# Position-weight sums by VectorE through DRAM, norm rows loaded inside the loop, high parts first: one change to a two-layer gMLP and mLSTM trunk

## The chip, the cores and the metric

The kernel runs on one core of a Trainium2 chip, in one launch. The metric is the device time of that launch in microseconds (us). A core has five engines with their own instruction streams: TensorE (PE in the profile; its weight loads are listed apart as PEld), VectorE (DVE), ScalarE (ACT), GpSimd (POOL) and SyncE (SP). SP does no arithmetic here; it issues nearly all DMA transfers, in order, and an instruction that waits holds up what stands behind it on its engine. On-chip memory has 128 partitions: tiles live in SBUF, and matmuls write to PSUM, which has eight banks.

## The reference

The input is 256 tokens of 1024 features in float32. Two layers follow one another. Layer 0 mixes tokens with a chunked causal gMLP, layer 1 with an mLSTM of 4 heads; after each come a SwiGLU block of width 2816 and a gated embedding. Every sub-block ends in a layer norm over alpha * x + y. The part that the change speaks of first is the gMLP:

```python
z = jax.nn.gelu(x @ w_in)
u, v = jnp.split(z, 2, axis=-1)
v = layer_norm(v, ln_g, ln_b)
ws = jnp.where(causal, w_s, jnp.zeros_like(w_s))
sv = jnp.einsum('gts,bcsgd->bctgd', ws, v) + b_s.T[:, :, None]
return (u * sv.reshape(B, S, GM_HALF)) @ w_out
```

There are 8 groups of 384 features, and chunks of 128 positions. Since v is normalised with gain and bias per feature, the kernel applies the position weights to the plain normalised v, scales by the gain, and adds bias times R plus b_s. R[g, t] is the sum of the masked position weights ws[g, t, s] over s.

## The kernel before

**Precision.** All products are made in float32 by pairs: a value is split into a high part (a cast to TensorE's float32r format) and a low part (what the cast leaves over). A product is then three matmuls: high by high, low by high, high by low. The helper `split` (L151) makes both parts, the cast on ScalarE (or on VectorE with `fast`) and the subtraction on VectorE. So each weight goes through four steps: a DMA into a tile `raw` (4 buffers), the cast and the subtraction into a tile `w` (6 buffers, or 8 wider ones), and the matmuls.

**The stream of weights.** `weight_plan` (L75) lists all weight tiles of 512 KB (a few are smaller) in the order of use. `ahead` (L170) issues loads up to 8 tiles ahead of use and splits up to 4 ahead; `weight` (L208) hands out the next tile. The loads are all issued by SP, L176. The first three weights are loaded and split by halves.

**The order of instructions.** The text gives each engine a program order, but a planner places the instructions: with its own estimate of times it lets a later instruction that could start go ahead of an earlier one that could not, and assigns buffers. `issue_after` holds a block's instructions behind a given one on the same engine, and `manual_schedule` keeps the text's order on the engines named.

**The start (L353 to L376).** Eight dummy matmuls warm TensorE up. x arrives transposed, in four tiles of two feature blocks (`xr`), and is split into `xh` and `xl`. The very first halves of x and of the first weight are cast by VectorE, the rest by ScalarE.

**The v phase (L379 to L412).** For six column groups c, the product x by the v half of w_in is accumulated over eight feature blocks k, for two token tiles t; then GELU and the statistics of the norm. At c = 4 the position weights arrive, transposed (`wsr`, s on the partitions, with t along the row); GpSimd zeroes the part over the diagonal, and they are split into `ws`. TensorE then multiplies a matrix of ones by them: each result has R for all t in every partition. ScalarE copies that into `R` (L393 to L398). `bs` is a row of 1024 values, spread over the partitions by its load. wsr, bs and R share three buffers with the tag "row", as the norm rows do.

**The u, gating and output loop (L482).** In step s, `u_block` makes 128 features of u, `sv_block` (L442) mixes positions for 128 features of v, and `acc.add` multiplies a finished block by w_out. In `sv_block` the moving operand has 256 columns, the high and the low part of `ws` side by side; there are two matmuls per token tile, one for the high part of v and one for its low part (L448). GpSimd makes `cf`, R times the bias plus b_s (L451, L452), and adds it.

**The channel mixer (L497), once in each layer.** `boundary` ends an accumulation with a layer norm, whose gain and bias are rows of 1024 that `load_row` (L347) spreads over the partitions, 512 KB each. `first` makes the first 512 features of gate and up by token tiles; the loop over f makes the others by `gate_up`, with `acc.add` of the down product two blocks behind. The rows for the second norm and for the embedding gate (g2, b2, bg, L582) are loaded, by the text, after that loop; the planner can place them earlier.

**The mLSTM's gates (L843 to L881).** After the q, k and v products come the gates of all heads: a short chain on VectorE and ScalarE over 4 partitions. Its results have to get to TensorE twice: `transpose_cols` (L860) turns them into columns, and `broadcast_gates` (L867) spreads G over the partitions with a 4-row selection matrix, two heads for each call. Both are put between the products of z block 10 (`z_mm(10, ...)`, L875): the number in the dictionary is the k before which a piece stands.

**The mLSTM's down product (L968 to L984).** `Down` accumulates into four PSUM banks, two for each token tile. At the beginning the first two blocks are multiplied for token tile 0, then for token tile 1; from f = 2 on, each block is done for both at once.

Of the kernel before, what the change touches and what calls it, by code (L numbers as in the profile page):

```python
# [133 lines left out]
def trunk(ctx, tc, a, out):  # L134
# [35 lines left out]
    def ahead(loads, casts):  # L170
        while at["load"] < min(len(plan), at["use"] + loads):
            ap = plan[at["load"]][1]
            n = ap.shape[-1]
            t = tl("raw", [P, n], name="raw")
            for c in HALF if at["load"] < 3 else [slice(0, n)]:
                sp.dma_start(t[:, c], ap[:, c])  # L176
                if at["load"] == 0 and c.start == 0:
                    second_x()
            raws[at["load"]] = t
            at["load"] += 1  # L180
        while at["cast"] < min(len(plan), at["use"] + casts):
# [12 lines left out]
            with issue_after(behind["cast"]):  # L194
# [6 lines left out]
                for c in () if key[0] == "bdv" else HALF if i < 3 else [slice(0, n)]:  # L201
                    split(t[:, 0, c], t[:, 1, c], raw[:, c], fast=i == 0 and c.start == 0)
# [156 lines left out]
    for i in range(4):  # L359
        t = tl("m2", [P, 2, S], name="xr")  # L360
        if i == 0:

            act.dma_start(t[:, 0, :], a["xT"][i, :, 0, :])
            second_x = lambda: sp.dma_start(xr[0][:, 1, :], a["xT"][0, :, 1, :])
            xr.append(t)
        else:
            sp.dma_start(t, a["xT"][i])
            xr.append(t)
        ahead(1 + i, int(i == 0))
    make_identity(nc, ident)  # L370
    pool.memset(mhalf, -0.5)
    for i in range(4):
        for k in ((0,), (1,)) if i == 0 else ((0, 1),):
            c, cr = slice(2 * i + k[0], 2 * i + k[-1] + 1), slice(k[0], k[-1] + 1)
            split(xh[:, c, :], xl[:, c, :], xr[i][:, cr, :], fast=c.start == 0)
            ahead(LOAD_AHEAD, 1 + i)  # L376

    vs = []
    for c in range(6):  # L379
        if c == 4:  # L380
# [11 lines left out]

            R = tl("row", [P, NG, P], name="R")  # L393
            for j in range(2):
                ps = bank("A", [P, 4, P], "rps")
                for i in range(2):
                    pe.matmul(ps, ones_r, ws[:, 4 * j:4 * j + 4, i, :], start=i == 0, stop=i == 1)
# [44 lines left out]
    def sv_block(f):  # L442
# [3 lines left out]
        for t in range(2):  # L446
            for i in range(2):
                pe.matmul(ps[:, t], v[:, i, t, c], ws[:, g], start=i == 0, stop=i == 1)  # L448
# [48 lines left out]
    def channel_mixer(l, acc, last, hook=None):  # L497
# [70 lines left out]
        transpose_h(0)  # L568
        for f in range(4, NF + LAG):
# [12 lines left out]
        g2, b2, bg = load_row(a["ln2_g"][l]), load_row(a["ln2_b"][l]), load_row(a["ple_b"][l])  # L582
# [94 lines left out]
    def mlstm(embed1):  # L677
# [156 lines left out]
        with tc.manual_schedule(engines={mybir.EngineType.Activation}):  # L834
# [32 lines left out]
            def broadcast_gates():  # L867

                gb = bank("A", [P, 2, 2, P], "gb")
                for h in range(2):  # L870
                    for i in range(2):
                        pe.matmul(gb[:, h], selH[:, 2 * len(gbs) + h, :], Gs[i], start=i == 0, stop=i == 1)
# [95 lines left out]
        acc = Down(NI)  # L968
        for h in range(NH):
# [22 lines left out]
def lay_out(inputs):  # L992
# [26 lines left out]
    def part(w):  # L1019
# [11 lines left out]
        "gm_wsT": i["gm_w_s"][0].transpose(2, 0, 1).reshape(P, NG * P),  # L1031
        "gm_bs": i["gm_b_s"][0].reshape(-1),
# [47 lines left out]
```

## Time and profile before

| What | Value |
|---|---|
| time before, median of 3 runs (lowest to highest) | 827.05 us (826.75 to 827.43) |
| profiled execution: its time, its span | 827.14 us, 825.4 us |
| granted TensorE clock in it | 0.999 |
| TensorE matmuls | 817.7 us busy, 4520 instructions |
| TensorE weight loads | 708.6 us |
| VectorE, ScalarE, GpSimd | 615.5, 471.4, 152.3 us |
| DMA | 155.52 MB, 188 GB/s on average |

The profile is of one execution. Its time and its span differ because the span runs from the first to the last instruction of the program. In a timeline row the columns are: start in us from the span's start, length in us (for several merged instructions, from the first start to the last end), engine, line of the kernel, operation, the tile written and the tiles read, shapes, and the number of instructions; in brackets stands the idle time of the engine before it and what ended it. A row with "q" at the engine is the engine's sequencer, such as SP issuing a DMA. In a row of waits come who waited, for whom, the total in us, the number of times and the longest. Matmuls overlap: each has a latency of its own, and the distance between two starts tells what one costs in a stream.

### The profile page before, as it was taken

The numbers are of one execution on the slowest core, as the hardware profiler recorded it, in microseconds if no ns is written. First come the engines' busy times: TensorE is split into PE (matmuls) and PEld (weight loads), VectorE is DVE, ScalarE is ACT, GpSimd is POOL, SyncE is SP. The second block draws the span as 40 slices with busy tenths as digits, with TensorE's granted clock in tenths as the row PEclk, the third lists the DMA queues.
The fourth block names the chain that finished last, engine by engine and source line by source line (L and its number), as shares of the span: only waits on it lengthen the run. The fifth ranks groups of instructions, "written<-read, shape, count | busy, mean of one in ns | idle before, by whom it ended". The sixth has DMA issues, their size and how long they took to land.

```text
span 825.4 us, 12401 instructions
## 1 busy us (share of the span) xinstructions
PE 817.7 (99%) x4520; PEld 708.6 (86%) x4520; DVE 615.5 (75%) x981; ACT 471.4 (57%) x819; POOL 152.3 (18%) x209
## 2 busy tenths in 40 slices
PE   9999999999999999999999999999999999999997
PEld 6888888888888888888889999998887888888886
DVE  6757998678956567596877998889785656776674
ACT  6656766565435556475256788776434555655522
POOL 1020633343000000700001777420000000000000
PEclk9999999999999999999999999999999999999999
DMA  8885456558286567577144454454636656886501
GB/s 303 277 329 179 153 169 215 179 183 290 93 282 196 179 192 261 185 250 235 47 135 160 134 165 154 166 180 151 229 124 220 195 180 193 257 247 220 179 1 52
DMA packets 44997, 155.52 MB, mean 188 GB/s; under 512 B 5256, under 2 KB 6024, under 8 KB 44936
## 3 DMA queue, kind: packets, MB, share of 16 engines
q1 hardware_dynamic: 44792, 154.60, 56.9%
q8 instruction: 35, 0.57, 0.3%
q14 instruction: 26, 0.21, 0.1%
q10 hardware_dynamic: 144, 0.13, 0.0%
HBM read 153.67 MB, written 1.05 MB: 187 GB/s over the span
## 4 chain that ended last, share of the span: by engine, by line
PE 95%; DVE 2%; DMA 1%; ACT 1%; issue 0%; SPq 0%; POOL 0%; DVEq 0%; ACTq 0%
PE acc L240 9%; PE acc L241 9%; PE acc L242 9%; PE pu L260 8%; PE pg L260 8%; PE ups L260 5%; PE pg L264 4%; PE pu L264 4%; PE ups L264 3%; PE vps L242 3%; PE vps L240 3%; PE vps L241 3%; PE xmps L245 2%; PE xmps L247 2%; PE xmps L246 2%; PE gate L289 2%
## 5 line engine op out<-in xcount | busy, mean ns | idle before, releaser
L153 DVE TENSOR_TENSOR w<-raw,w 128x1024 fp32r<-128x1024 f32 (+1 forms) x279 | 336.1, 1212 | 74.2 <-ACT w L153 72.9
L153 ACT CAST w<-raw 128x1024 fp32r<-128x1024 f32 (+1 forms) x278 | 286.6, 1042 | 118.9 <-PE acc L242 23.5
L240 PE MATMUL acc<-w,h 128*128 128x512 f32 x336 | 131.8, 392 | 0.2 <-ACT hn L943 0.2
L241 PE MATMUL acc<-w,h 128*128 128x512 f32 x336 | 131.4, 391 | 0.0
L242 PE MATMUL acc<-w,h 128*128 128x512 f32 x336 | 130.8, 389 | 0.0
L242 PEld LDWEIGHTS acc<-w,h 128*128 128x128 f32 x336 | 63.1, 188 | 13.6
L240 PEld LDWEIGHTS acc<-w,h 128*128 128x128 f32 x336 | 63.2, 188 | 12.3 <-ACT hn L943 0.6
L241 PEld LDWEIGHTS acc<-w,h 128*128 128x128 f32 x336 | 63.2, 188 | 10.9
L260 PE MATMUL pg<-xs,w 128*128 128x512 f32 x288 | 71.6, 391 | 0.0
L260 PE MATMUL pu<-xs,w 128*128 128x512 f32 x288 | 71.5, 390 | 0.0
L260 PEld LDWEIGHTS pg<-xs,w 128*128 128x128 f32 x288 | 53.8, 188 | 11.0
L260 PEld LDWEIGHTS pu<-xs,w 128*128 128x128 f32 x288 | 53.8, 188 | 11.0
L319 POOL TENSOR_TENSOR rs<-ve,mhalf 128x1 f32<-128x1 f32 x8 | 7.6, 956 | 297.3 <-DVE ve L318 292.8
L271 ACT COPY s<-pg 128x256 f32<-128x256 f32 x36 | 13.4, 372 | 73.3 <-PE pg L264 73.3
L272 DVE TENSOR_TENSOR s<-s,pg 128x256 f32<-128x256 f32 x36 | 15.1, 421 | 45.5 <-ACT s L271 45.4
L260 PE MATMUL ups<-xs,w 128*128 128x512 f32 x192 | 47.7, 391 | 0.0
L260 PEld LDWEIGHTS ups<-xs,w 128*128 128x128 f32 x192 | 35.7, 188 | 7.2
L264 PEld LDWEIGHTS pg<-xs,w 128*128 128x128 f32 x288 | 38.9, 188 | 3.1
L264 PE MATMUL pg<-xs,w 128*128 128x256 f32 x288 | 39.5, 280 | 0.0
L264 PE MATMUL pu<-xs,w 128*128 128x256 f32 x288 | 39.4, 279 | 0.0
L240 PE MATMUL vps<-w,xs 128*128 128x512 f32 x96 | 37.6, 392 | 0.5 <-DVE w L153 0.5
L241 PE MATMUL vps<-w,xs 128*128 128x512 f32 x96 | 37.5, 390 | 0.0
(245 smaller groups left out, 1625.6 us busy)
## 6 DMA issues: line engine op xcount, KB each, us to landing
raw<-in_ffn_g SPq DMA_DIRECT2D x44, 512.0 KB, 4.3
raw<-in_ffn_u SPq DMA_DIRECT2D x44, 512.0 KB, 4.3
raw<-in_ffn_d SPq DMA_DIRECT2D x44, 512.0 KB, 4.4
raw<-in_gm_u SPq DMA_DIRECT2D x24, 512.0 KB, 3.4
raw<-in_gm_wo SPq DMA_DIRECT2D x24, 512.0 KB, 3.3
raw<-in_gm_v SPq DMA_DIRECT2D x21, 512.0 KB, 4.9
raw<-in_ple_gate SPq DMA_DIRECT2D x16, 512.0 KB, 4.5
raw<-in_ml_z SPq DMA_DIRECT2D x16, 512.0 KB, 3.6
```

What stands on the lines that cost most here:

```text
L153: return dve.tensor_copy(hi, src) if fast else act.copy(hi, src), sub.tensor_tensor(lo, src, hi.bitcast(F32), ALU.subtract)
L240: pe.matmul(ps, lh, w[:, 0, c], start=start, stop=False)
L241: pe.matmul(ps, ll, w[:, 0, c], start=False, stop=False)
L242: pe.matmul(ps, lh, w[:, 1, c], start=False, stop=stop)
L245: pe.matmul(ps, w[:, 0, c], h, start=start, stop=False)
L246: pe.matmul(ps, w[:, 0, c], l, start=False, stop=False)
L247: pe.matmul(ps, w[:, 1, c], h, start=False, stop=stop)
L260: pe.matmul(ps, w[:, 0, k * P:(k + 1) * P], xs[:, k], start=k == 0, stop=False)
L264: pe.matmul(ps[:, 0], w[:, 1, k * P:(k + 1) * P], xh[:, k, :], start=False, stop=k == KD - 1)
L271: act.copy(o, ps[:, 1])
L272: dve.tensor_tensor(o, o, ps[:, 0], ALU.add)
L289: pe.matmul(ps, xl[:, k, TOK[t]], w[:, 0, c], start=False, stop=k == KD - 1)
```

## The change

1. **R.** The position weights are also loaded untransposed at c = 3 (`wsn`, t on the partitions). GpSimd zeroes the part over the diagonal, VectorE sums over s into a tile `Rt` of 128 x 8, a DMA issued by GpSimd writes this to a DRAM scratch `Rd` (8 x 128), and a second one loads it back, spread over the partitions, into `R`. The four matmuls by ones and the two copies of ScalarE go.
2. **Gating.** The matmul of v's low part takes only the high part of `ws`: 128 columns instead of 256. The product of the two low parts is left out.
3. **Norm rows.** g2, b2 and bg are loaded at f = 8, 10 and 12 inside the loop, each held on SP behind the weight load issued last.
4. **Gates.** The transposes stand before k = 2 instead of 1; the broadcasts of all four heads stand before k = 4, in one piece, instead of two before k = 4 and k = 7.
5. **Start.** On ScalarE and VectorE the splits of the first four blocks of x and of the first two weights are in an order written out by hand, with the casts shared out differently; in the first four blocks of the first product, each block's high by high matmuls come first, for both token tiles, then low by high, then high by low.
6. **Down product of the mLSTM.** It begins with three blocks for token tile 0, then three for token tile 1.

The core of the diff:

```diff
@@ trunk
+    with tc.manual_schedule(engines={mybir.EngineType.Activation, mybir.EngineType.DVE}):
+        for i in range(2):
+            w, raw = tl("w", [P, 2 * D + P], F32R, "w")[:, :2 * D].rearrange("p (i n) -> p i n", i=2), raws.pop(i)
+            for k, h in enumerate(HALF):
+                c = 2 * i + k
+                act.copy(xh[:, c], xr[i][:, k])
+                if k == 0:
+                    dve.tensor_copy(w[:, 0, h], raw[:, h])
+                else:
+                    act.copy(w[:, 0, h], raw[:, h])
+                dve.tensor_tensor(xl[:, c], xr[i][:, k], xh[:, c].bitcast(F32), ALU.subtract)
+                dve.tensor_tensor(w[:, 1, h], raw[:, h], w[:, 0, h].bitcast(F32), ALU.subtract)
+            wt[i] = w
...
     for c in range(6):
+        if c == 3:
+            wsn = tl("row", [P, NG, P], name="wsn")
+            sp.dma_start(wsn, a["gm_ws"].rearrange("p (g s) -> p g s", g=NG))
+            pool.affine_select(
+                out=wsn, in_=wsn, compare_op=ALU.is_ge, fill=0.0, base=0, pattern=[[0, NG], [-1, P]], channel_multiplier=1
+            )
+            Rt = tl("c", [P, NG], name="Rt")
+            dve.tensor_reduce(Rt, wsn, mybir.AxisListType.X, ALU.add)
+            Rd = ctx.enter_context(tc.tile_pool(name="dr", bufs=1, space=bass.MemoryType.DRAM)).tile([NG, P], F32, name="Rd")
+            pool.dma_start(Rd.rearrange("g t -> t g"), Rt)
+            R = tl("row", [P, NG, P], name="R")
+            pool.dma_start(R, Rd.rearrange("g t -> (g t)").partition_broadcast(P).rearrange("p (g t) -> p g t", g=NG))
...
-            R = tl("row", [P, NG, P], name="R")
-            for j in range(2):
-                ps = bank("A", [P, 4, P], "rps")
-                for i in range(2):
-                    pe.matmul(ps, ones_r, ws[:, 4 * j:4 * j + 4, i, :], start=i == 0, stop=i == 1)
-                act.copy(R[:, 4 * j:4 * j + 4, :], ps)
...
+                if c == 0 and k < 4:
+                    for x, i in ((xh, 0), (xl, 0), (xh, 1)):
+                        for t in range(2):
+                            pe.matmul(ps[t], x[:, k, TOK[t]], w[:, i, HALF[kk]], start=k == 0 and x is xh and i == 0, stop=False)
+                    continue
@@ sv_block
-            for i in range(2):
-                pe.matmul(ps[:, t], v[:, i, t, c], ws[:, g], start=i == 0, stop=i == 1)
+            pe.matmul(ps[:, t], v[:, 0, t, c], ws[:, g], start=True, stop=False)
+            pe.matmul(ps[:, t, 0], v[:, 1, t, c], ws[:, g, 0], start=False, stop=True)
@@ channel_mixer
+            if f in (8, 10, 12):
+                with issue_after([at["dma"]]):
+                    rows.append(load_row(a[("ln2_g", "ln2_b", "ple_b")[f // 2 - 4]][l]))
...
-        g2, b2, bg = load_row(a["ln2_g"][l]), load_row(a["ln2_b"][l]), load_row(a["ple_b"][l])
+        g2, b2, bg = rows
@@ mlstm
-                gb = bank("A", [P, 2, 2, P], "gb")
-                for h in range(2):
+                gbs.extend(bank("A", [P, 2, 2, P], "gb") for _ in range(2))
+                for h in range(NH):
                     for i in range(2):
-                        pe.matmul(gb[:, h], selH[:, 2 * len(gbs) + h, :], Gs[i], start=i == 0, stop=i == 1)
-                gbs.append(gb)
-            z = z_mm(10, {1: transpose_cols, 4: broadcast_gates, 7: broadcast_gates})
+                        pe.matmul(gbs[h // 2][:, h % 2], selH[:, h, :], Gs[i], start=i == 0, stop=i == 1)
+            z = z_mm(10, {2: transpose_cols, 4: broadcast_gates})
...
-                if f == 0:
-                    first = block
-                elif f == 1:
-                    for t in range(2):
-                        for b, h2, w in (first, block):
+                if f < 3:
+                    begin.append(block)
+                    for t in range(2) if f == 2 else ():
+                        for b, h2, w in begin:
                             acc.mm(b, t, h2, w)
```

More of the change, by code (lines that the diff above doesn't have):

```diff
@@ L201, in ahead @@
                 for c in () if key[0] == "bdv" else HALF if i < 3 else [slice(0, n)]:
-                    split(t[:, 0, c], t[:, 1, c], raw[:, c], fast=i == 0 and c.start == 0)
+                    split(t[:, 0, c], t[:, 1, c], raw[:, c])
             wt[i] = t
@@ L368, in trunk @@
             xr.append(t)
-        ahead(1 + i, int(i == 0))
+        ahead(1 + i, 0)
     make_identity(nc, ident)
     pool.memset(mhalf, -0.5)
[L372 to L376, printed above, removed]
+    with tc.manual_schedule(engines={mybir.EngineType.Activation, mybir.EngineType.DVE}):
[11 more added lines that the diff above has]
+            wt[i] = w
+    at["cast"] = 2
+    for i in range(2, 4):
+        c = slice(2 * i, 2 * i + 2)
+        split(xh[:, c, :], xl[:, c, :], xr[i])
+        ahead(LOAD_AHEAD, 1 + i)
     vs = []
     for c in range(6):
+        if c == 3:
[10 more added lines that the diff above has]
+            pool.dma_start(R, Rd.rearrange("g t -> (g t)").partition_broadcast(P).rearrange("p (g t) -> p g t", g=NG))
         if c == 4:
@@ L568, in channel_mixer @@
         transpose_h(0)
+        rows = []
         for f in range(4, NF + LAG):
@@ L968, in mlstm @@
         acc = Down(NI)
+        begin = []
         for h in range(NH):
```

3 lines of the change are left out of this document (2 added, 1 removed).

## The prediction

> **What bounds the kernel now.** I read the page's totals first, then TensorE's waits, then the timeline around each place that the diff touches. Three lines of the page: the span, the engines' busy times, the DMA packets of the main queue.
>
> ```profile
> span 825.4 us, 12401 instructions
> PE 817.7 (99%) x4520; PEld 708.6 (86%) x4520; DVE 615.5 (75%) x981; ACT 471.4 (57%) x819; POOL 152.3 (18%) x209
> q1 hardware_dynamic: 44792, 154.60, 56.9%
> ```
>
> TensorE works through the whole span; beside its own weight loads (86%) no engine is above 75%. So an edit counts by what it takes from TensorE's stream, or from the few moments in which that stream stands. All such moments after the start, by TensorE's waits:
>
> ```profile
> PE first L286 <- ACT w L153: 1.1, 1, 1.1
> PE acc L240 <- ACT hn L943: 0.2, 1, 0.2
> PE cp L863 <- DVE gt L853: 0.2, 1, 0.2
> ```
>
> They are short, and the listed wait understates each, because matmuls overlap: a row of a matmul lasts 0.39 us, while the next one starts 0.23 us later. I therefore cost everything by the distance from start to start. The profiled execution took 827.14 us, that is 1.74 us around its span and 0.09 us above the median of 827.05; I sum against 827.14 and take 0.09 off.
>
> **Part 1, the sums R.** The ones-matmuls in TensorE's timeline, and the first matmul behind them:
>
> ```profile
> 49.59 1.07 PE L397 MATMUL rps<-ws,ones_r 128*128 128x512 f32 x4
> 50.50 0.39 PE L240 MATMUL vps<-w,xs 128*128 128x512 f32 x1
> ```
>
> Four matmuls go, 50.50 - 49.59 = **0.91 us** (0.228 for each of 512 columns). Nothing waited for them or made them wait, so this is plain. Two copies by ScalarE go too, which is worth nothing: ScalarE is 57% busy. In their place come: a 512 KB load on SP's queue, a select of 128x1024 by GpSimd, a sum of 128x1024 by VectorE, a write of 1024 single 4-byte elements to DRAM and a 512 KB spread load, both issued by GpSimd. Rows that bound them, in order: the select of the same size, VectorE's pass of that size, the first use of R's products, the landing times of the row loads, and the issue and first use of the first u weight.
>
> ```profile
> 41.83 1.11 POOL L383 TENSOR_SCALAR_AFFINE_SELECT wsr<-wsr 128x1024 f32<-128x1024 f32 x1 [38.61 <-DMA wsr<-in_gm_wsT]
> L153 DVE TENSOR_TENSOR w<-raw,w 128x1024 fp32r<-128x1024 f32 (+1 forms) x279 | 336.1, 1212 | 74.2 <-ACT w L153 72.9
> 83.05 1.29 POOL L457 TENSOR_TENSOR sv<-sv,cf 128x256 f32<-128x256 f32 x1 [7.00 <-ACT sv L456]
> DMA to landing us min/median/max: 3.6/5.9/8.0
> 49.41 0.33 SPq L176 DMA_DIRECT2D raw<-in_gm_u  x1
> 72.42 1.82 PE ups L260 x8
> ```
>
> I let the new load take the place of wsr, so that the data are there at 41.8; the select takes 1.1, the sum about 1.2 (VectorE's mean for a pass over 128x1024), so 44.2. The write has no row like it. Lower bound 3.6 us, the shortest row load. Upper: 56.9% of 16 engines' 825.4 us over 44792 packets is 0.168 us a packet; 1024 packets on 16 engines are then 10.7 us, and 8.0 for landing. The spread load is 3.6 to 8.0. R lands between 51 and 71, nearer 55, as the two are ordinary small and large transfers; it is needed at 83. Cost zero, covered by 12 us at worst. The new waits: GpSimd stands before the spread load until the write has landed; behind it are the select of wsr, the cf products and at 83.05 the first sum, nothing else. VectorE's sum waits for the select; behind it are weight splits, and SP's load of bs waits for that sum because there are only three row buffers, with weight loads behind it. TensorE uses the first u weight 23 us after its load was issued, so delays of some us there are absorbed.
>
> **Part 2, the narrower gating matmuls.** 48 matmuls (24 blocks, two token tiles) go from 256 columns to 128. TensorE's and the weight loads' timeline; the first two rows are today's svps block and its successor, the others a place where a 272-column and a 136-column matmul alternate already:
>
> ```profile
> 80.58 0.64 PE L448 MATMUL svps<-ws,vn 128*128 128x256 f32 x4
> 81.05 0.86 PE L260 MATMUL ups<-xs,w 128*128 128x512 f32 x3
> 457.68 0.23 PE L775 MATMUL vps<-w,xm 128*128 128x136 f32 x1
> 457.74 0.34 PE L774 MATMUL vps<-w,xm 128*128 128x272 f32 x1
> 457.91 0.23 PE L775 MATMUL vps<-w,xm 128*128 128x136 f32 x1
> 457.68 0.19 PEld L774 LDWEIGHTS vps<-w,xm 128*128 128x128 f32 x1
> 457.79 0.19 PEld L775 LDWEIGHTS vps<-w,xm 128*128 128x128 f32 x1
> ```
>
> Today a 256-column matmul takes (81.05 - 80.58)/4 = 0.118 us. By columns, 128 would take 0.06, and indeed 457.74 - 457.68 = 0.06 behind the short one. But the long one behind it then stands 0.17 instead of 0.12: the pair takes 457.91 - 457.68 = 0.23, since the next weights cannot follow sooner than 457.79 - 457.68 = 0.11. A short matmul thus costs what a weight load costs, 0.11, and saves about 0.01: **0.5 us** in 48. Bounds: 0.3 (the pair at 0.23 against 0.236) and 48 x 0.06 = 2.9. I stay near the row with the same pattern. By the Trainium skill, "TensorE: Matmul & The Clock Gate", section "Back-to-back issue gap", a stream of load and matmul pairs sustains about 81 ns per matmul at 128 columns; by that this part would be an estimated 1.8 us. The trace disagrees with its 0.11, and the measurement decides.
>
> **Part 3, the norm rows.** SP's queue, the chain that ended last, TensorE in the second channel mixer, and the usual landing of such a weight:
>
> ```profile
> 611.78 0.33 SPq L349 DMA_DIRECT2D row<-in_ln_b  x1
> 612.57 0.33 SPq L349 DMA_DIRECT2D row<-in_ple_b  x1
> 613.70 5.96 DMA raw<-in_ffn_u
> 619.75 1.05 ACT w L153
> 619.31 0.39 PE L286 MATMUL first<-w,xs 128*128 128x512 f32 x1
> 620.84 0.50 PE L286 MATMUL first<-w,xs 128*128 128x512 f32 x1 [1.14 <-ACT w L153]
> 621.18 0.40 PE L287 MATMUL first<-w,xs 128*128 128x512 f32 x1
> raw<-in_ffn_u SPq DMA_DIRECT2D x44, 512.0 KB, 4.3
> ```
>
> Two row loads of 512 KB go out just before a weight that is already late (it had to wait for a buffer), and it lands after 5.96 us where 4.3 is usual; ScalarE's split of 1.05 follows. TensorE loses 620.84 - 619.31 - 0.23 = 1.3 us, and 0.1 more at the restart (621.18 - 620.84 = 0.34 for 0.23). With the rows gone from there the weight lands after 3.6 (the quickest row load, of the same size) to 4.3, at 617.3 to 618.0; the split ends by 619.1, before the 619.54 at which TensorE would want it, and the weights behind it are for later tiles. Gain **1.4 us**; zero if the landing still takes 5.9. The three loads of each layer (0.33 of issue each) now stand in SP's queue behind a weight of f = 8, 10 and 12, with the next weights behind them. TensorE has no wait in that loop and the transfers fill 57% of the engines' time; cost zero, cover the weights' lead; without it 0.33 and about 1.5 of transfer each. In the first layer the same move finds no stall to remove.
>
> **Part 4, the gate transposes and broadcasts.** TensorE in the z product of block 10:
>
> ```profile
> 528.39 0.28 PE L863 MATMUL cp<-ident,gt 4*128 4x4 f32 x2
> 528.84 0.28 PE L863 MATMUL cp<-ident,gt 4*128 4x4 f32 x2 [0.17 <-DVE gt L853]
> 530.10 0.28 PE L247 MATMUL zps<-xs,w 128*128 128x256 f32 x1
> 530.31 0.73 PE L872 MATMUL gb<-G,sel 4*128 4x256 f32 x4
> 531.20 0.28 PE L246 MATMUL zps<-xs,w 128*128 128x256 f32 x1
> ```
>
> One position later means three matmuls of 0.118 later, 0.35 us. The second pair stood 0.45 behind the first, with 0.17 of listed idle time; 0.35 later it finds its operand. A wait costs more than is listed (part 3); I take 0.23, half of the 0.45. A change to the four-row broadcasts and back costs: from 530.10 to 531.20 are six matmuls, 0.71 by columns but 1.10 in fact, so 0.39 per visit, and one of two visits goes. Together **0.6 us**, between 0 and 0.7.
>
> **Part 5, the start.** VectorE, ScalarE and TensorE, the first weights:
>
> ```profile
> 4.48 0.29 DVE L153 CAST xs<-xr 128x256 fp32r<-128x256 f32 x1 [3.03 <-DMA xr<-in_xT]
> 4.69 0.42 DVE L153 CAST w<-raw 128x512 fp32r<-128x512 f32 x1
> 5.17 0.50 PE L240 MATMUL vps<-w,xs 128*128 128x512 f32 x1 [0.50 <-DVE w L153]
> 7.94 1.32 ACT L153 CAST w<-raw 128x512 fp32r<-128x512 f32 x2
> 8.61 0.50 PE L240 MATMUL vps<-w,xs 128*128 128x512 f32 x1
> 11.52 0.39 PE L240 MATMUL vps<-w,xs 128*128 128x512 f32 x1
> ```
>
> VectorE makes both first casts one after the other; now ScalarE makes that of x, so the first matmul can start 0.2 earlier, and with the high products first the low parts are wanted 0.45 later each. That alone is not kept: the second weight's cast starts at 7.94, and TensorE goes on only at 8.61. VectorE's cast of a half (0.42) in place of ScalarE's (1.32 for two, 0.66) brings this to 8.4. From 8.61 to the 25th matmul at 11.52 another 0.18 is lost against twelve of 0.228. I take **0.25 us**; bounds: the 0.9 by which 24 matmuls exceed 24 x 0.228, and a loss of 0.1, one more restart, should a low part now be late.
>
> **Part 6, three blocks ahead in the down product:** zero, at most 0.4 (the wait on hn above). TensorE's order here is the planner's, not the text's, and I expect it to fill this wait as before.
>
> Sum: 0.91 + 0.5 + 1.4 + 0.6 + 0.25 = 3.66 us; 827.14 - 3.66 - 0.09 = **823.4 us**.
>
> **Rivals.** *The late weight stays late* (other transfers fill the gap, or the planner moves something else there): 1.4 less, 824.8. For it: the load starts only when a buffer is freed. Against: 5.96 is the outlier beside 4.3.
>
> *Short matmuls cost by columns*: 2.4 more than taken, 821.0. The start 0.06 behind the short one speaks for it, the 0.17 behind the next against. The figure of the Trainium skill in part 2 points this way; by it the whole would be an estimated 822.1.
>
> *R comes late, the kernel gets slower.* Place: the cf products that GpSimd must finish before 83.05. If the two transfers issued by GpSimd need over 39 us together (44.2 to 83), every us more is a us of TensorE's; at 43 the gain is gone, and at 46 the time is 830.4. For it: the trace has no transfer issued by GpSimd. Against: 27 us is the most that I can derive. By the Trainium skill, "SBUF — State Buffer", section "SBUF: two separate sides", GpSimd writes such a transfer's descriptors and is locked out while VectorE runs a two-port operation, for which a copy of f32 qualifies; no run here shows it yet.
>
> *The planner's new order opens other waits*, of the size of the 1.3 us one, in two or three places: 826 to 828, no change that can be told.
>
> **How the numbers follow.** Forecast 0.52, weight still late 0.20, by columns 0.08, R late 0.08, new waits 0.12. About 0.2% (1.65 us) is what a measurement of this kernel can tell from no change. Forecast, late weight and columns are faster, 0.80; new waits 0.12 the same; R late 0.08 slower. The range goes from 820.7, 0.3 under the columns' case, to 825.9, the sum of the lower bounds (827.05 - 0.91 - 0.3 + 0.1): it holds 0.80.
>
> **What would show it.** Right: no rps matmuls; svps pairs at 0.23 and weight loads 0.11 apart; no wait of "first" on w; one visit of gb; cp without a wait; TensorE's 25th matmul near 11.3. Wrong: svps pairs at 0.18, a wait of GpSimd's cf on R past 83, a new line above 0.5 us in TensorE's waits.

## The result, and the profile after

The changed kernel takes 835.41 us (median of 4 runs, 834.44 to 835.84); the kernel before took 826.90 us beside it (4 runs, 826.73 to 827.43). The ratio is 1.0095, with a 95% interval from 1.0083 to 1.0108: **slower by about 8.5 us**, where 823.4 us had been forecast. The profiled execution took 835.21 us, its span is 833.5 us.

The page's totals, span and busy times of the engines, after:

```profile
span 833.5 us, 12406 instructions
PE 820.8 (98%) x4516; PEld 710.4 (85%) x4516; DVE 614.5 (74%) x983; ACT 469.5 (56%) x818; POOL 152.3 (18%) x212
```

Four matmuls are gone, and yet TensorE is listed as 3.1 us busier. Matmuls that only run longer at a lower clock count as busy, so this line alone does not say where the time went. TensorE's waits do, in part (who waited for whom, total, times, longest, in us):

```profile
PE vps L240 <- ACT w L153: 3.1, 1, 3.1
PE svps L475 <- DVE vn L153: 2.1, 1, 2.1
PE vps L242 <- DVE w L153: 0.7, 1, 0.7
PE num L946 <- POOL plo L153: 0.4, 1, 0.4
```

The wait of `first` on a weight (1.1 us before) and the one of `cp` (0.2 us) have gone, as the prediction said. Four new lines have come. To place the whole difference I compared the starts of the same matmuls in the two timelines of TensorE:

| Stretch | Change in this stretch, us |
|---|---|
| up to the 25th projection product (vps) | -0.06 |
| to the last projection product | +5.21 |
| to the first mixing product (svps) | +0.05 |
| to the third block's mixing products | +4.05 |
| to the last block's mixing products | -0.12 |
| to the mLSTM's gate products | +0.13 |
| to the first head's products with V (num) | -0.65 |
| to the second head's | +0.65 |
| to the end of the second channel mixer's first part | -1.57 |
| to the end of the span | +0.38 |

The mixing products come in blocks of four. The sum is 8.07 us, the difference of the spans (833.5 and 825.4) up to rounding. Two stretches make the loss, and both lie between 65 and 96 us.

**The first stall.** TensorE's timeline after (start, length, engine, line, operation; in brackets the idle time and what ended it):

```profile
65.69 0.39 PE L242 MATMUL vps<-w,xs 128*128 128x512 f32 x1
69.22 0.50 PE L240 MATMUL vps<-w,xs 128*128 128x512 f32 x1 [3.15 <-ACT w L153]
69.56 0.40 PE L241 MATMUL vps<-w,xs 128*128 128x512 f32 x1
70.67 0.50 PE L242 MATMUL vps<-w,xs 128*128 128x512 f32 x1 [0.72 <-DVE w L153]
71.01 0.57 PE L240 MATMUL vps<-w,xs 128*128 128x512 f32 x1
```

From start to start, where 0.23 is usual, it loses 69.22 - 65.69 - 0.23 = 3.30 us and 70.67 - 69.56 - 0.23 = 0.88 us, and 0.11 us at each of the two restarts (69.56 - 69.22 and 71.01 - 70.67 are 0.34). Then the clock drops. Busy time by stretches (bounds in us, length, then each engine's busy time; granted clock, DMA share and GB/s stand last):

```profile
71.00:74.40 3.40, 3.40 (x10) 2.63 (x9) 3.40 (x5) 2.32 (x5) 0.00 (x0) 0.51 0.82 251
74.40:77.00 2.60, 2.60 (x13) 2.13 (x12) 1.96 (x2) 0.70 (x1) 0.00 (x0) 0.99 0.89 296
88.20:89.10 0.90, 0.84 (x3) 0.74 (x4) 0.90 (x4) 0.51 (x1) 0.00 (x0) 0.50 0.75 105
89.10:91.40 2.30, 2.30 (x7) 1.82 (x8) 2.30 (x5) 1.78 (x4) 0.00 (x0) 0.50 0.53 198
```

3.4 us at a granted clock of 0.51 are 1.7 us lost. Together that is 6.1 us; less the removed products' 0.9 it is the +5.21 of the table.

What was late is the cast of a weight on ScalarE. GpSimd's timeline after shows what ScalarE was behind:

```profile
43.79 1.14 POOL L405 DMA_DIRECT2D Rd<-Rt  x1 [1.56 <-DVE Rt L403]
55.84 0.58 POOL L407 DMA_DIRECT2D R<-Rd  x1 [10.91 <-DMA Rd<-Rt]
64.30 1.79 POOL L478 TENSOR_SCALAR cf<-R,gmp 128x128 f32<-128x128 f32 x3 [7.88 <-DMA R<-Rd]
66.05 1.09 POOL L411 TENSOR_SCALAR_AFFINE_SELECT wsr<-wsr 128x1024 f32<-128x1024 f32 x1
```

GpSimd writes the sums at 43.79, stands 10.91 us until they have landed, issues the spread load, stands 7.88 us again until that has landed, because the planner has put the first `cf` products next, and only then comes to the select of wsr, at 66.05 where it stood at 41.83 before. GpSimd's order is not all of that delay. The load of wsr went out later as well, in two views (SP's queue; size and us to landing):

```profile
46.75 0.42 SPq L410 DMA_DIRECT2D wsr<-in_gm_wsT  x1
wsr<-in_gm_wsT SPq DMA_DIRECT2D x1, 512.0 KB, 14.2
```

It was issued at 34.77 before. Now it lands at 60.98, so the select could not have run sooner than that, and the last 5.07 us are GpSimd's order. ScalarE's timeline after:

```profile
56.98 1.05 ACT L153 CAST w<-raw 128x1024 fp32r<-128x1024 f32 x1 [6.59 <-DMA raw<-in_gm_v]
67.18 1.04 ACT L153 CAST ws<-wsr 128x1024 fp32r<-128x1024 f32 x1 [9.15 <-POOL wsr L411]
68.13 2.94 ACT L153 CAST w<-raw 128x1024 fp32r<-128x1024 f32 x3
```

ScalarE works in order. Its next instruction was the cast of ws, which nobody needed before 85 us; behind it stood three casts of weights, the first of which TensorE wanted at 65.9 us. So the wait went from GpSimd (and the late wsr) to ScalarE to the weights to TensorE.

**The second stall.** The chain that ended last, after, leads to it (start, length, what; rows left out are marked):

```profile
72.91 6.33 DMA raw<-in_gm_u
...
79.34 1.06 ACT w L153
...
80.42 1.23 DVE w L153
81.65 1.20 DVE sums L439 x2
...
83.34 1.77 POOL vrs L319 x2
...
87.61 0.61 DVE vn L153
...
88.26 0.47 PE svps L475
```

A weight of the u phase lands late, since its buffer came free late. ScalarE casts it, and the subtraction stands in VectorE's queue ahead of the statistics of v; behind these stand the normalisation and the split of v, for which the first mixing product with v's low part waits. It starts at 88.26, 2.48 us behind its predecessor at 85.78 instead of 0.12, and the clock is 0.50 again in the last two rows of stretches above. That is 2.4 us of waiting and 1.6 us of half clock (3.2 us at 0.50), the +4.05 of the table.

**The transfers in the meantime.** The same stretch, 47 to 55 us, of the kernel before and of the changed one (the last three numbers: granted clock, DMA share, GB/s):

```profile
47.00:55.00 8.00, 8.00 (x37) 6.63 (x36) 4.99 (x6) 5.22 (x7) 3.95 (x6) 1.00 0.81 288
```

```profile
47.00:55.00 8.00, 8.00 (x37) 6.63 (x36) 3.08 (x4) 2.25 (x3) 0.00 (x0) 1.00 0.44 36
```

While the write of 4 KB is under way the core moves 36 GB/s instead of 288. The landing times of the weights issued between 45 and 52 us, before and after:

```profile
DMA to landing us min/median/max: 4.1/5.7/7.3
```

```profile
DMA to landing us min/median/max: 11.7/11.8/16.9
```

So the trace offers two causes, the order of the work (GpSimd's, and with it the late load of wsr) and the slow transfers, and one cannot tell from it what each is worth.

### The profile page after: what moved, and what is told of

Read it like the earlier page. It is cut to its first block, busy times and chain, and to the rows that moved or that the text cites. A ratio compares the mean times of both kernels' runs of the same rounds, so it can differ in the third digit from the quotient of the medians.

```text
span 833.5 us, 12406 instructions
## 1 busy us (share of the span) xinstructions
PE 820.8 (98%) x4516; PEld 710.4 (85%) x4516; DVE 614.5 (74%) x983; ACT 469.5 (56%) x818; POOL 152.3 (18%) x212
## 4 chain that ended last, share of the span: by engine, by line
PE 86%; DMA 4%; DVE 3%; issue 3%; ACT 2%; POOL 1%; SPq 0%; DVEq 0%; ACTq 0%; POOLq 0%
PE acc L240 9%; PE acc L241 9%; PE acc L242 9%; PE pu L260 8%; PE pg L260 8%; PE ups L260 5%; PE pg L264 4%; PE pu L264 4%; PE ups L264 2%; DMA raw<-in_gm_v 2%; PE xmps L245 2%; PE xmps L246 2%; PE xmps L247 2%; PE gate L289 2%; PE gate L287 2%
## 5 line engine op out<-in xcount | busy, mean ns | idle before, releaser
L260 PEld LDWEIGHTS pu<-xs,w 128*128 128x128 f32 x288 | 53.8, 188 | 11.0
L240 PE MATMUL vps<-w,xs 128*128 128x512 f32 x88 | 35.0, 398 | 3.1 <-ACT w L153 3.1
L264 PEld LDWEIGHTS pu<-xs,w 128*128 128x128 f32 x288 | 36.5, 188 | 0.3
```

The source lines that it names most:

```text
L240: pe.matmul(ps, lh, w[:, 0, c], start=start, stop=False)
L260: pe.matmul(ps, w[:, 0, k * P:(k + 1) * P], xs[:, k], start=k == 0, stop=False)
L264: pe.matmul(ps[:, 0], w[:, 1, k * P:(k + 1) * P], xh[:, k, :], start=False, stop=k == KD - 1)
```

## The experiments

**Theory:** two causes together, no third. The select, with ScalarE's cast and the weights behind it, stands behind GpSimd's waits; and the write of single elements slows all other transfers. **Rivals:** one of the two alone; GpSimd as the issuer of the transfers; other parts of the change. Ratios below are to the kernel before on the same chip.

### Part 1 undone

```diff
-        if c == 3:
-            wsn = tl("row", [P, NG, P], name="wsn")
...
+            R = tl("row", [P, NG, P], name="R")
+            for j in range(2):
+                ps = bank("A", [P, 4, P], "rps")
...
```

> The changed kernel with part 1 undone: R by the ones-matmuls as before, all other parts kept. Both theories: no wait of TensorE over 1 us in the v and u phases. By the distances between landmarks in the two traces the other parts are worth 1.3 to 1.7 us: 825.2 to 825.7. By the terms of the prediction (0.5 + 1.4 + 0.6 + 0.25) it would be 824.2.

Measured: 825.51 us (825.22 to 826.03), ratio 0.9985 (0.9975 to 0.9994). Without part 1 neither of the two stalls is there, and the rest of the change gains 0.15%. All of the loss is in part 1.

### The order alone

The spread load goes from c = 3 to c = 4 and is issued behind the select of wsr.

```diff
-            R = tl("row", [P, NG, P], name="R")
-            pool.dma_start(R, Rd.rearrange("g t -> (g t)").partition_broadcast(P).rearrange("p (g t) -> p g t", g=NG))
...
-            pool.affine_select(
+            sel = pool.affine_select(
...
+            R = tl("row", [P, NG, P], name="R")
+            with issue_after([sel]):
+                pool.dma_start(R, Rd.rearrange("g t -> (g t)").partition_broadcast(P).rearrange("p (g t) -> p g t", g=NG))
```

> The changed kernel, but GpSimd issues R's spread load behind the select of wsr instead of before it. Theory Q (the queues): GpSimd's select of wsr stood behind the wait for R, ScalarE's cast of ws waited for that select until 67.2 us, and the weight casts stood behind it. Then TensorE's waits of 3.1 us (on a weight) and 2.1 us (on vn) are gone or under 1 us together, and the time is 824.5 to 826. Rival T (the transfers): the write of single elements holds the DMA engines, the weights themselves land too late, and TensorE still waits: 831 or more, with the cast of ws done early and the next weight cast waiting for its DMA.

Measured: 831.02 us (827.13 to 832.76), ratio 1.0043 (1.0030 to 1.0055): the time is that of the second expectation, though the first stall goes, as the first had it. Two of TensorE's waits of this kernel:

```profile
PE svps L476 <- DVE vn L153: 2.1, 1, 2.1
PE svps L475 <- ACT vn L153: 0.5, 1, 0.5
```

The first stall is gone: the projection products end 0.81 us sooner than before the change. The second is there as it was, +4.1 us in the same stretch, and 0.7 us more are lost ahead of the first mixing product. The order explains one stall, not both. The edit moved more than GpSimd's work: the planner let SP issue the load of wsr at 36.30 instead of 46.75, so "order" stands for both here and below.

### The write alone in another layout

The scratch has t outside, so that each partition writes one run of 32 bytes: 128 runs instead of 1024 single elements. GpSimd reads the loaded sums with a stride of 8.

```diff
-            Rd = ctx.enter_context(tc.tile_pool(name="dr", bufs=1, space=bass.MemoryType.DRAM)).tile([NG, P], F32, name="Rd")
-            pool.dma_start(Rd.rearrange("g t -> t g"), Rt)
+            Rd = ctx.enter_context(tc.tile_pool(name="dr", bufs=1, space=bass.MemoryType.DRAM)).tile([P, NG], F32, name="Rd")
+            pool.dma_start(Rd, Rt)
...
-            R = tl("row", [P, NG, P], name="R")
+            R = tl("row", [P, P, NG], name="R")
...
-        pool.tensor_scalar(cf, R[:, g], gmp[:, f, 1:2], None, ALU.mult)
+        pool.tensor_scalar(cf, R[:, :, g], gmp[:, f, 1:2], None, ALU.mult)
```

> The changed kernel with the scratch laid out as 128 x 8, so that the write is 128 runs of 32 bytes instead of 1024 single elements; R is then read with a stride of 8 elements by GpSimd. If the number of elements made the write slow, it lands in 3 to 5 us instead of 11.8, weights issued meanwhile land in 4 to 7 us instead of 12 to 17, R is there near 53, and no stall of TensorE over 1 us is left: 824.5 to 826. If it is the issue by GpSimd that is slow, the write still takes over 8 us and the time stays above 831.

Measured: 826.63 us (825.08 to 828.02), ratio 0.9993 (0.9984 to 1.0003). The write lands after 2.54 us instead of 11.75, and the weights issued between 45 and 52 us after 3.4 to 10.2 us, which is not quite the 4 to 7 us expected. The stretch of the transfers in this kernel:

```profile
47.00:55.00 8.00, 8.00 (x37) 6.63 (x36) 5.07 (x6) 3.19 (x4) 0.55 (x1) 1.00 0.91 299
```

Most of the loss goes, though ScalarE still stands 8.30 us before the cast of ws. Two waits of 0.6 and 0.5 us stay in the mixing blocks, and the time lies above the 824.5 to 826 that was expected. Its runs spread over 3 us, so 826.63 is less firm than the others.

### Both

> Two edits at once: the scratch is written in runs of 32 bytes instead of single elements, and the spread load of the sums is issued by GpSimd behind the select of the mixing weights. Nothing is left out of the computation of the changed kernel. Two causes (the element-wise write slows the weight transfers beside it; the select, and with it ScalarE's cast, stands behind GpSimd's wait for the scratch), and no third: no stall of TensorE before the first mixing product, weights land in 4 to 7 us, and the 0.91 us of the removed products come through, so 825.5 of the kernel without this part less 0.9 = 824.6 us (824.3 to 825.0). Rival, the chain behind the last projection product (activation, statistics, normalisation, split) sets the start of the mixing products, and the removed products only moved its wait: about 825.5 us, with a wait of TensorE on DVE vn or ACT vn of 0.5 us or more. Rival, a strided read of the sums on GpSimd costs the mixing blocks something: a wait on DVE sv of about 0.5 us as in the run with the contiguous scratch alone, 825.1 us.

Measured: 825.07 us (824.85 to 825.62), ratio 0.9974 (0.9964 to 0.9984). TensorE's waits after the start:

```profile
PE num L947 <- POOL plo L153: 0.4, 1, 0.4
PE acc L240 <- ACT hn L975: 0.2, 1, 0.2
```

No stall is left before or in the mixing products, and the stretch from the 25th to the last projection product is 0.86 us shorter than before the change: the 0.91 of the prediction does come when nothing gives it back. The time itself lies just above the 824.3 to 825.0 that was expected. The rival of the strided read, which had 825.1, falls all the same: there is no wait on sv. The four kernels as a table, ratio to the kernel before:

| | spread load ahead of the select | behind it |
|---|---|---|
| 1024 single elements | 1.0095 | 1.0043 |
| 128 runs of 32 bytes | 0.9993 | 0.9974 |

The layout is worth 1.0% with the first order and 0.7% with the second; the order 0.5% and 0.2%. Each alone costs, and the two make each other worse; for the order alone the 0.2% is hardly more than the intervals allow (0.9984 to 1.0003 beside 0.9964 to 0.9984).

### The write issued by ScalarE

```diff
-            pool.dma_start(Rd.rearrange("g t -> t g"), Rt)
+            act.dma_start(Rd.rearrange("g t -> t g"), Rt)
```

> The changed kernel with the write of the scratch, single elements as they are, issued by ScalarE instead of GpSimd. If the number of elements makes it slow: it still takes over 8 us, the weights issued just behind it land in 10 us or more, and the time is above 831. If the issue by GpSimd is what is slow: it lands in 3 to 5 us and the time is 824.5 to 827.

Measured: 833.92 us (2 runs, 833.65 and 834.19), ratio 1.0084 (1.0064 to 1.0104). The write takes 10.73 us. Its queue and the stretch of the transfers in this kernel, in two views (queue: packets, MB, share of 16 engines from 44 to 56 us):

```profile
q10 hardware_dynamic: 1040, 0.00, 4.9%
```

```profile
47.00:55.00 8.00, 8.00 (x37) 6.61 (x36) 3.38 (x4) 2.25 (x3) 0.15 (x1) 1.00 0.78 41
```

From ScalarE's queue the same 4 KB are 1040 packets, about one for each element, and the other transfers are as slow, 41 GB/s. So it is the layout and not GpSimd as the issuer. The Trainium skill says as much of both: "DMA: Bandwidth & Descriptors", section "Rules for kernel authors", that a strided last dimension becomes one descriptor per element, and section "Issuing engines are not separate DMA queues", that transfers of all issuers run on the same 16 engines. The packets counted here, and the equal rates from either issuer, agree. GpSimd's queue lists the same write of the changed kernel in fewer packets (same window):

```profile
q0 software_dynamic: 32, 0.00, 3.3%
```

Both hold the same 1024 elements, so it is not the number of listed packets that makes the transfers slow.

### The write with nobody waiting for it

Part 1 undone, and beside that a write of the same form, from the statistics of v, which nobody reads.

```diff
+        if c == 3:
+            Rd = ctx.enter_context(tc.tile_pool(name="dr", bufs=1, space=bass.MemoryType.DRAM)).tile([NG, P], F32, name="Rd")
+            pool.dma_start(Rd.rearrange("g t -> t g"), sums[:, 10:18])
```

> The changed kernel with the sums made by TensorE again (part 1 undone), and beside that a transfer that nobody waits for: GpSimd writes 1024 single elements of the statistics to a scratch in DRAM at the place where the changed kernel writes the sums. Nothing of the computation is left out; the written data are read by nobody. If the element-wise write slows the other queues' transfers by itself: its landing takes 11 to 12 us, the weights issued behind it land in 11 to 17 us instead of 3 to 8, the u weights come late to ScalarE's cast, and TensorE waits before the first mixing products: 825.5 plus 2.5 to 4, that is 828 to 829.5 us. If the late landings in the changed kernel came from the spread load or from the order of the queues: 825.5 us and weights in 4 to 8 us.

Measured: 826.12 us (825.52 to 826.66), ratio 0.9986 (0.9977 to 0.9995). The mechanism is there, in the two views used above:

```profile
DMA to landing us min/median/max: 12.4/13.9/15.3
```

```profile
47.00:55.00 8.00, 8.00 (x37) 6.60 (x37) 3.96 (x5) 3.96 (x6) 4.07 (x6) 1.00 0.82 50
```

But the price is not: ratio 0.9986 beside 0.9985 without the write, and 0.5 us of waiting on sv where 2.5 to 4 us were expected. Its profiled execution, at 826.57 one of its longer runs, takes 1.2 us more from the first to the last mixing block than that of the kernel without the write. So the weights' lead swallows most of a late landing of some 14 us. In the kernel with the order put right SP issued three more weight tiles of v behind the write, the last at 50.46 us, and came to the u weights at 51.59; in this one it issued two and came to the u weights by 49.14 us. Part 1 also brings 512 KB of wsn, the select and sum that wait for it, and the spread load of R, another 512 KB. I take the shorter lead for the reason why the same write costs 5.5 us there (831.02 against 825.51). That is read from the issue times: no run varied the lead alone, and none left the spread load out.

### The norm rows alone

The kernel before with part 3 only.

```diff
...
+            if f in (8, 10, 12):
+                with issue_after([at["dma"]]):
+                    rows.append(load_row(a[("ln2_g", "ln2_b", "ple_b")[f // 2 - 4]][l]))
...
-        g2, b2, bg = load_row(a["ln2_g"][l]), load_row(a["ln2_b"][l]), load_row(a["ple_b"][l])
+        g2, b2, bg = rows
```

> The kernel before with one part of the change alone: the three norm rows of each layer loaded in the loop. Nothing is left out. The prediction put 1.4 us on it, the trace of the changed kernel showed a step of 1.54: 825.4 us (825.2 to 825.7). If that is so, this part alone gives all that the change without part 1 gave (825.51), and narrow products, start, gates and down blocks together give nothing. If it depends on the other parts, 826 or more.

Measured: 825.84 us (825.68 to 826.40), ratio 0.9985 (0.9976 to 0.9994), the ratio of the change without part 1. So of that change the rows give all that shows in the time; parts 2, 4, 5 and 6 together give nothing that does.

### The start and the gates undone

Both on the kernel with both edits.

```diff
-    with tc.manual_schedule(engines={mybir.EngineType.Activation, mybir.EngineType.DVE}):
...
+    for i in range(4):
+        for k in ((0,), (1,)) if i == 0 else ((0, 1),):
...
-                if c == 0 and k < 4:
...
```

> The same two edits, and the start as it was before the change (part 5 undone). Nothing is left out. Prediction's term for the start: 0.25 us, so 825.3 us. The traces showed the 25th projection product between 11.2 and 12.1 us in seven executions, old start and new start alike, so that the part may be worth nothing: 825.1 us, and more than 0.5 us slower only if the old start is worse than the first trace showed.

Measured: 825.13 us (824.63 to 825.70), ratio 0.9977 (0.9967 to 0.9987), beside 0.9974: the start is worth nothing that shows.

```diff
...
-            z = z_mm(10, {2: transpose_cols, 4: broadcast_gates})
+            z = z_mm(10, {1: transpose_cols, 4: broadcast_gates, 7: broadcast_gates})
```

> The same two edits, and the gates broadcast in two steps as before the change (part 4 undone). Nothing is left out. If the gain of the joined gates is all given back at the wait for plo, as the steps of the trace have it: no change, 825.1 us, and from the first gates to the second head's products the trace shows the same time. If the prediction's term held: 0.6 us slower, 825.7 us.

Measured: 825.04 us (824.49 to 825.54), ratio 0.9974 (0.9964 to 0.9985), the same as with the joined gates, and without the wait for plo.

### The new wait for plo

The changed kernel's wait, in TensorE's and in GpSimd's timeline:

```profile
544.98 0.40 PE L945 MATMUL num<-vn,phi 128*128 128x512 f32 x1
545.78 0.50 PE L946 MATMUL num<-vn,plo 128*128 128x512 f32 x1 [0.41 <-POOL plo L153]
```

```profile
543.67 2.05 POOL L153 TENSOR_TENSOR plo<-sc,phi 128x384 fp32r<-128x384 f32 x1 [11.39 <-ACT phi L153]
```

TensorE is there 0.65 us sooner, and the subtraction on GpSimd, which hung on other engines, is not. Two ways out were tried. First, on the kernel with part 1 undone, the first head's subtraction on VectorE:

```diff
-                split(hi, lo, p, sub=pool)
+                split(hi, lo, p, sub=dve if h == 0 else pool)
```

> The changed kernel with the sums made by TensorE again (part 1 undone), and the low part of the first head's weights p subtracted on VectorE instead of GpSimd; nothing is left out. If the gain of the moved gates was lost to the 2.04 us subtraction on GpSimd alone: the wait of TensorE for plo (0.5 us) goes, and the kernel is 0.5 to 0.7 us faster than without this edit, 824.9 us. If VectorE's own queue (a weight split of 1.2 us ahead of the next head) is as late, a wait of 0.2 to 0.5 us stays or the next head's low part waits instead: 825.3 to 825.6 us.

Measured: 829.15 us (827.09 to 830.73), ratio 1.0022 (1.0012 to 1.0031), 3.6 us slower than without the edit. Neither expectation was right. The wait for plo is gone, and in TensorE's waits stands instead:

```profile
PE acc L240 <- ACT hn L967: 2.1, 1, 2.1
PE num L937 <- ACT e L912: 0.9, 1, 0.9
```

The planner has made another order of it. ScalarE casts one more weight ahead of the second head's phi and stands 1.3 us for that weight's landing, so all heads come later: the pattern of the first stall again. Behind the wait on hn the granted clock is 0.50 for 3.4 us.

Second, TensorE's order instead of the engine, on the kernel with both edits: in the first head all products of the high part of p come first.

```diff
+            for part in ("hi", "lo") if h == 0 else ("both",):
...
+                        if part != "lo":
+                            pe.matmul(num[t], hi[:, c], vn[h][:, 0, s, :], start=first, stop=False)
+                            pe.matmul(num[t], hi[:, c], vn[h][:, 1, s, :], start=False, stop=False)
+                        if part != "hi":
+                            pe.matmul(num[t], lo[:, c], vn[h][:, 0, s, :], start=False, stop=end)
...
```

> The changed kernel with the scratch in runs of 32 bytes and the spread load behind the select (the two edits that removed the stalls), and in the first head's products with V those of the low part of p behind all of those of the high part: four products of some 0.23 us each are put in front of the wait for plo. Nothing is left out. If the new wait for plo (0.4 us and 0.65 us in the step) is what took back the gain of the gates and PE's order is all that changes: 825.07 - 0.65 = 824.4 us, and TensorE waits for plo no more. If the order of VectorE and ScalarE moves with it, as it did when that subtraction was moved to VectorE, a wait on phi, e or hn of later heads takes its place: 825.0 us or more.

Measured: **824.25 us** (824.14 to 824.68), ratio 0.9964 (0.9950 to 0.9977). TensorE's timeline of this kernel:

```profile
535.76 0.40 PE L948 MATMUL num<-vn,phi 128*128 128x512 f32 x1
536.00 0.85 PE L950 MATMUL num<-vn,plo 128*128 128x512 f32 x3
```

No gap. The stretch from the first to the second head's products is 0.67 us shorter than with both edits alone, and 0.28 us of it goes at the wait on hn (0.5 us instead of 0.2). This is the fastest kernel measured here, 0.36% under the kernel before, and 0.8 to 0.9 us under the two of the section above, which were measured beside it. The interval of its ratio still overlaps theirs, so that this edit gains is shown by the trace and the medians, not by the intervals. Nothing in it is left out beyond what the change left out.

## Why the prediction was wrong

**Part 1, the failed step.** It said that behind GpSimd's wait stand "the select of wsr, the cf products and at 83.05 the first sum, nothing else", and gave this "cost zero, covered by 12 us at worst". The list stopped at GpSimd's own instructions. The select has a reader, ScalarE's cast of ws, and behind that one, in order, stand the casts of weights. Nor did it ask where the load of wsr would go when it let "the new load take the place of wsr": 12 us later in SP's queue. The cover was not the 83 us at which R is needed but the 65.9 us at which TensorE wanted the next weight. The durations held: the write took 11.75 us within the bounds of 3.6 and 18.7, the spread load 8.37 where at most 8.0 was allowed, and R landed at 64.21 within "51 and 71". R was never late. What lay behind the wait was. That the write lay near the 10.7 us worked out for its packets is luck: at ScalarE's queue 4.9% of 16 engines over 12 us are 9.4 us for 1040 packets, 0.009 us for each and not 0.168, so the packets' own time does not explain the landing.

The second half of the same step: the write got a price for itself and none for the transfers beside it. They fell to 36 GB/s and weights landed after 11.7 to 16.9 us. The sentence that "delays of some us there are absorbed" holds, to within about 1 us, for the write alone; in the changed kernel it is false, and with the order put right too. A gain of 0.91 us became a loss of 9.3 in the two stretches. The gain itself was sized right: 0.86 to 0.91 us in the four kernels with both edits.

**The rivals.** That the kernel gets slower was one of them, by the wrong mechanism. It was to decide once GpSimd's two transfers take more than 39 us together; they took 11.75 + 8.37 = 20.1 us, and the kernel was slower all the same. The sentence on descriptors that VectorE locks out was not needed either: issued by ScalarE, the write took 10.73 us. Nearest in kind was the last rival, new waits in two or three places; it held them to be of 1.3 us and the time to be 826 to 828, and had neither the half clock behind them nor a cause.

**Part 2, mis-sized.** 0.5 us forecast, 0.12 measured from the third to the last gating block. TensorE's timeline after, one block and the next product:

```profile
105.57 0.28 PE L474 MATMUL svps<-ws,vn 128*128 128x256 f32 x1
105.69 0.22 PE L475 MATMUL svps<-ws,vn 128*128 128x128 f32 x1
105.75 0.34 PE L474 MATMUL svps<-ws,vn 128*128 128x256 f32 x1
105.92 0.23 PE L475 MATMUL svps<-ws,vn 128*128 128x128 f32 x1
105.98 0.45 PE L240 MATMUL acc<-w,h 128*128 128x512 f32 x1
106.27 0.39 PE L241 MATMUL acc<-w,h 128*128 128x512 f32 x1
```

The pattern is the predicted one: 0.06 behind a short matmul, then 0.17 for the long one. Four take 105.98 - 105.57 = 0.41 instead of 0.47. But the successor of the last short one, with 512 columns, pays too: it stands 106.27 - 105.98 = 0.29 before the next one, where 0.23 is usual. I had counted pairs and not what follows the row of four.

**Part 3, right.** 1.4 us forecast, 1.54 in the step and 0.15% measured alone; the wait of `first` is gone.

**Part 4, right and given back.** 0.6 us forecast, 0.65 in the step, 0.65 returned at plo. The failed step is not a size: I did not ask whether what TensorE reaches sooner is ready sooner. GpSimd's row ends at 543.67 + 2.05 = 545.72, and TensorE got there at 545.2.

**Part 5, mis-sized.** The first matmul starts 0.40 us earlier, and by the 25th 0.06 us is left. In the eleven other kernels' executions the 25th stands between 11.06 and 12.08 us, with the old start (11.48, 12.08) and the new one alike. The 0.25 us was smaller than what one execution's start differs from another's.

**Part 6, right:** zero. The kernel with the norm rows alone, which has not got this part, shows the same step of 1.57 us.

**The end, not foreseen.** The last 0.38 us of the table lie behind the issue of the last store: from there the span runs on for 2.7 us before the change and 3.1 after. Of the twelve executions the eight with part 1's two transfers have 0.24 to 0.39 us there, the one with the write alone 0.12, and the three without either at most 0.02. So it goes with these transfers; why, was not tried.

## What to carry to other kernels

Where a change adds a wait, follow it through every queue: not only what stands behind the waiting instruction, but who reads that, and what stands behind the reader on its own engine. A small transfer can cost more than its time: ask into how many pieces it falls, and what is under way beside it. And a piece of time taken from the engine that sets the end counts only if what this engine reaches next is ready sooner as well.

## What the runs showed of the hardware

- A write of 4 KB as 1024 single elements takes 10.7 to 13.3 us to land and holds the rate of all transfers at 23 to 50 GB/s for that time (four kernels, 47 to 55 us), where 235 to 313 are moved in the nine kernels without it; as 128 runs of 32 bytes it takes 2.5 to 3.2 us (five kernels). Its packets' own time is small: 0.7 to 4.0% of 16 engines' time over 12 us in the three kernels where GpSimd issues it, 4.9% where ScalarE does.
- After a long enough wait TensorE runs at half clock. The changed kernel has 3.4 us at 0.51 behind the first stall, whose longest gap is 3.53 us from start to start, and another 3.4 us at 0.50 around the end of a gap of 2.48 us. In all kernels here there are five gaps of 2.45 us or more behind the start, and half clock follows each, for 3.4 us in four cases and for 6.8 us in the kernel with ScalarE's write; none follows the other gaps, of which the longest that stands alone is the 1.53 us before `first` in the kernel before. The Trainium skill, "TensorE: Matmul & The Clock Gate", section "Part 1: The HAM clock gate (the "warmup" mystery)", has a window of about 3.4 us, and the length at half clock agrees with it. It lets the clock fall after an idle window of that length; here gaps of 2.45 to 2.53 us did it too.
